# A state-space stage on one core: where the split of a quarter's result stands in the program

## The chip, the core and the metric

The kernel runs on one core of a Trainium2 chip as one launch. The metric is the device time of the whole kernel in microseconds (us). The engines are named as in the profile: PE (TensorE, matrix products), PEld (its weight loads), DVE (VectorE), ACT (ScalarE), POOL (GpSimd) and SP (SyncE, which here issues the DMAs). Each engine takes its instructions strictly in the order of its own list and waits where one is not ready; so an instruction that waits holds up all that stand behind it on that engine.

## The reference

One layer of a decoder trunk over 1024 tokens with 1024 channels, in float32. An input projection feeds three mixers side by side; their gated sum and a feed-forward part follow. Cut to what matters here:

```python
h = rms_norm(x, mix_norm_g[i])
(u, c_b, c_c, c_x, q, k_c, ..., mix_gates) = split_projection(h @ w_in[i])
y_ssm  = s5_mixer(u, ...)      # this change is inside the kernel's stage for it
y_conv = short_conv_mixer(c_x, c_b, c_c, conv_w[i], conv_w_out[i])
y_attn = nsa_mixer(q, ...)
mixed = gates[:, :, 0] * y_ssm + gates[:, :, 1] * y_conv + gates[:, :, 2] * y_attn

def s5_mixer(...):
    bu = einsum('bsgh,gph->bsgp', uf, b_bar)
    _, states = associative_scan(combine, (a, bu), axis=1)
    y = einsum('bsgp,ghp->bsgh', states, c).real + d_skip * uf
    y = gelu(y)
    y_lin, y_gate = split(y @ w_glu, 2)
    return y_lin * sigmoid(y_gate)
```

## The kernel before

Every float32 product is done as three products of two-part operands: a value is split into a rounded high part and a low remainder (`split`: the high part is one copy on ACT, line 61; the low part is one subtraction on DVE, line 62). In the trace these are `whi`, `wlo` for weights (from a page `raw` loaded by DMA) and `mhi`, `mlo` for moving operands. `prod` (lines 120, 122, 124) is the loop of three products. SBUF is cut into 44 pages of 128x1024 floats that are handed out in turn; a new holder of a page waits until the last reader of the old one is done. PE writes to four one-bank accumulators `acc` and two double ones `wide`.

The state-space mixer runs in four quarters of 128 channels, q = 0 to 3 (`s5`). A quarter, in the order of the program:

- `s5_kernel` (line 979 on): a short convolution kernel M, whose Toeplitz form is made by eight small DMAs `M<-kz` (line 991); `s5_carry`: four DMAs `cp<-cr`.
- `s5_back` (lines 1079 to 1085): the result of the quarter before, which `s5_out` had written to DRAM (`sy<-YN`), comes back transposed in eight DMAs `yT<-sy` (line 1084).
- `s5_inputs` (line 1002 on): eight transposes on PE and two copies on ACT make `Bm`.
- `s5_parts` (lines 1087 to 1091): the two-part split of `yT`, one ACT copy `mhi<-yT` and one DVE subtraction `mlo<-yT`. Its result is read only after all four quarters, by the products of `mix_ssm`.
- `s5_scan`: sixteen products `wide<-UT,Bm` (line 1015); copies of them into a page V, two on DVE (line 1024) and two on ACT (1022); then on DVE rotations and two rounds of four scans (lines 1031, 1033, 1035, 1039), and rotations back into `X` (lines 1048, 1050, 1054).
- `s5_tables` (lines 903 to 957) on DVE for the next quarter, and `s5_out`: products of M and of X (lines 1066, 1070) and a GELU on ACT (`YN`, line 1073).

Between these steps `beat` and `fill` put products of other mixers, one at a time, into PE's list: the short convolution (weights times `hh`, `hl`; evacuations `cb`, `z`, `cv` on ACT, products `z<-z,cb` and `cv<-cv,cy` on POOL, taps `cy` on DVE), then `u_block(3)` (the input of quarter 3), then `mix_plain` for the convolution branch (needs `mhi<-cv`, `mlo<-cv`; each accumulator is evacuated on DVE by line 1166, `m<-gp,acc`) and for the attention branch (needs `mhi<-oraw`, `mlo<-oraw`; evacuated as `gp<-gp,acc`). PE's order is written out by hand (`manual_schedule`); a list scheduler orders the other engines by program order and readiness.

```python
def s5_parts(self):
    hi, lo = self.page("mhi", F32R), self.page("mlo", F32R)
    cut = lambda x: x.rearrange("p (n t) -> p n t", t=8)
    self.split(cut(hi), cut(lo), self.last.rearrange("p t n -> p n t"))
    self.yT.append((hi, lo))
```

Of the kernel before, what the change touches and what calls it, by code (L numbers as in the profile page):

```python
# [33 lines left out]
class Trunk:  # L34
# [203 lines left out]
    def kv_rows(self):  # L238
# [7 lines left out]
        W = [self.weights() for _ in range(5)]  # L246
        A, B = (W[0], W[2]), (W[1], W[3], W[4])
        for t in range(NT):
            ps = self.wide()
            tok = slice(t * P, (t + 1) * P)  # L250
            for k in range(KD):
                a, b = A[k // 4], B[k // 3]
                ca, cb = slice((k % 4) * 256, (k % 4) * 256 + 256), slice((k % 3) * 280, (k % 3) * 280 + 280)
# [16 lines left out]
            nc.vector.tensor_tensor(sq[:, :256], kr, kr, op=OP.mult)  # L270
            nc.vector.tensor_reduce(self.ssk[:, t], sq[:, :256].rearrange("p (n d) -> p n d", d=64), axis=AX.X, op=OP.add)
            if t > 4:
# [34 lines left out]
    def q_rows(self):  # L307
# [3 lines left out]
        for t in range(NT):  # L311
# [8 lines left out]
            nc.vector.tensor_tensor(sq, q, q, op=OP.mult)  # L320
            nc.vector.tensor_reduce(self.ssq[:, t], sq.rearrange("p (n d) -> p n d", d=64), axis=AX.X, op=OP.add)
            self.q.append(q)
# [41 lines left out]
    def compress(self):  # L364
# [27 lines left out]
        for which in range(2):  # L392
# [25 lines left out]
            nc.vector.tensor_tensor(sv, kv, kv, op=OP.mult)  # L418
            nc.vector.tensor_reduce(ss, sv, axis=AX.X, op=OP.add)
            self.rstd(ss)  # L420
# [39 lines left out]
    def cmp_scores(self, t):  # L460
# [11 lines left out]
        m, sm = st[:, 0:8], st[:, 8:16]  # L472
        nc.vector.tensor_reduce(m, v, axis=AX.X, op=OP.max)
        nc.vector.tensor_tensor(v, v, m[:, :, None].to_broadcast([P, 8, 32]), op=OP.subtract)
        nc.scalar.activation(v, v, AF.Exp)
        nc.vector.tensor_tensor(v, v, self.seen[:, t, None, :].to_broadcast([P, 8, 32]), op=OP.mult)
        nc.vector.tensor_reduce(sm, v, axis=AX.X, op=OP.add)
        nc.vector.tensor_scalar(sm, sm, 1e-30, None, op0=OP.max)
# [199 lines left out]
    def u_block(self, q, beside=None):  # L678
# [9 lines left out]
        nc.sync.dma_start(spill, ut)  # L688
        self.U[q] = U = self.page("UT").rearrange("p (g n) -> p g n", g=8)
        nc.sync.dma_start(U, spill.rearrange("(g h) j n -> (h j) g n", g=8))  # L690

    def u_blocks(self):

        self.tab, self.U = {}, {}

# [299 lines left out]
    def s5_inputs(self, q, bp):  # L995

        nc = self.nc
        B = self.page("Bm").rearrange("p (a g c s) -> p a g c s", a=4, g=2, c=2)
        ps = self.wide()
# [4 lines left out]
        for c in range(2):  # L1004
            nc.scalar.activation(B[:, :, :, c], ps.rearrange("p (j c g s) -> p c j g s", j=4, c=2, g=2)[:, c], AF.Copy)
        self.fill(2 * self.F5)
        return B

    def s5_scan(self, q, U, B, ep):
        nc = self.nc  # L1010
        v = nc.vector
        V = self.page("V5").rearrange("p (c a n) -> p c a n", c=2, a=4)
        ps = self.wide()
        for j in range(8):
            nc.tensor.matmul(ps[:, j * P:(j + 1) * P], B[:, j // 2, j % 2].rearrange("p c s -> p (c s)"), U[:, j],
                             start=True, stop=True)
        pv = ps.rearrange("p (a g n) -> p g a n", a=4, g=2)
        for g in range(2):
            for c in range(2):
                o = V[g * 64:(g + 1) * 64, c]  # L1020
                if c:
                    nc.scalar.activation(o, pv[c * 64:(c + 1) * 64, g], AF.Copy)
                else:
                    nc.vector.tensor_copy(o, pv[c * 64:(c + 1) * 64, g])
        self.fill(2 * self.F5)
        f = lambda x: x.rearrange("p a n -> p (a n)")
        vr, vi, ec, es = f(V[:, 0]), f(V[:, 1]), f(ep[:, 0]), f(ep[:, 1])
        t = [self.half("m5") for _ in range(3)]
        a, b = self.half("a5"), self.half("b5")
        for o, z, x0, x1, op in ((b, t[2], vi, vr, OP.subtract), (a, t[0], vr, vi, OP.add)):  # L1030
            v.tensor_tensor(z, x0, ec, op=OP.mult)
            self.beat()
            v.tensor_tensor(t[1], x1, es, op=OP.mult)
            self.beat()
            v.tensor_tensor(z, z, t[1], op=op)
            self.beat()
            for j in range(4):
                s = slice(j * P, (j + 1) * P)
                v.tensor_tensor_scan(o[:, s], self.mag8[:, 4 * q + j:4 * q + j + 1].to_broadcast([P, P]), z[:, s], 0.0,
                                     op0=OP.mult, op1=OP.add)  # L1040
                if j % 2:
                    self.beat()
        X = self.page("X5").rearrange("p (a g n) -> p a g n", a=4, g=2)
        nc.gpsimd.memset(X[:, :, :, 0:1], 0.0)
        w = lambda x: x.rearrange("p (a n) -> p a n", a=4)[:, :, 0:127]
        ec, es = ep[:, 0, :, 0:127], ep[:, 1, :, 0:127]
        for c, x0, x1, op in ((0, a, b, OP.subtract), (1, b, a, OP.add)):
            v.tensor_tensor(w(t[0]), w(x0), ec, op=OP.mult)
            self.beat()
            v.tensor_tensor(w(t[1]), w(x1), es, op=OP.mult)  # L1050
            self.beat()
            for g in range(2):
                pr = slice(g * 64, g * 64 + 64)
                v.tensor_tensor(X[c * 64:(c + 1) * 64, :, g, 1:], w(t[0])[pr], w(t[1])[pr], op=op)
                self.beat()
        return X

    def s5_out(self, q, U, M, X, cp):

        nc = self.nc  # L1060
        Y = self.page("YN")
        ps = self.wide()
        for half in range(2):
            b = ps[:, half * 512:half * 512 + 512]
            for j in range(4):
                nc.tensor.matmul(b[:, j * P:(j + 1) * P], M[:, half * 2 + j // 2, j % 2], U[:, half * 4 + j],
                                 start=j == 0, stop=False, skip_group_check=True)
            for j in range(4):
                a, g = half * 2 + j // 2, j % 2
                nc.tensor.matmul(b[:, j * P:(j + 1) * P], cp[:, a, g], X[:, a, g], start=False, stop=j == 3,  # L1070
                                 skip_group_check=True)
            self.fill(self.F5)
        nc.scalar.activation(Y, ps, AF.Gelu_apprx_tanh)
        self.fill(2 * self.F5)
        self.spill_y = spill = self.dram.tile([P, 8, P], F32, tag=f"sy{q}", name=f"sy{q}")
        nc.sync.dma_start(spill, Y.rearrange("p (g n) -> p g n", g=8))
# [25 lines left out]
    def s5(self):  # L1102
        self.yT = []
        tab = self.tab
        for q in range(4):
            bp, cr, bb, ep = tab.pop(q)
            M = self.s5_kernel(q, cr, bb)
            cp = self.s5_carry(cr)
            U = self.U[q]
            if q:  # L1110
                self.s5_back()
            B = self.s5_inputs(q, bp)
            if q:
                self.s5_parts()
            self.F5B = 3.5 if q < 3 else 5
            X = self.s5_scan(q, U, B, ep)
            if q < 3:
                for _ in self.s5_tables(q + 1, tab):
                    self.beat()
            self.fill(self.F5S)  # L1120
            self.s5_out(q, U, M, X, cp)
        self.fill(16)
        self.s5_back()
        self.fill(16)
        self.s5_parts()
# [661 lines left out]
```

## Time and profile before

| | us |
|---|---|
| median of 3 runs (1775.83 to 1778.55) | 1776.4 |
| profiled execution: time | 1776.64 |
| profiled execution: span from first to last instruction | 1774.7 |
| PE busy in the span | 1736.4 (98%) |
| DVE busy | 1202.1 (68%) |
| ACT busy | 794.7 (45%) |

The profiled execution takes 1.9 us more than its span and stands 0.2 us above the median. PE is busy nearly all the time, so the time goes down only where PE waits or where its granted clock is at the lower of its two levels; mean granted clock 0.993 of full. A row of the timeline gives start, duration, engine, line, operation, operands, the count, and in brackets how long the engine was idle before it and what ended that.

### The profile page before, as it was taken

The numbers are of one execution on the slowest core, as the hardware profiler recorded it, in microseconds if no ns is written. First come the engines' busy times: TensorE is split into PE (matmuls) and PEld (weight loads), VectorE is DVE, ScalarE is ACT, GpSimd is POOL, SyncE is SP. The second block draws the span as 40 slices with busy tenths as digits, with TensorE's granted clock in tenths as the row PEclk, the third lists the DMA queues.
The fourth block names the chain that finished last, engine by engine and source line by source line (L and its number), as shares of the span: only waits on it lengthen the run. The fifth ranks groups of instructions, "written<-read, shape, count | busy, mean of one in ns | idle before, by whom it ended". The sixth has DMA issues, their size and how long they took to land.

```text
span 1774.7 us, 23597 instructions
## 1 busy us (share of the span) xinstructions
PE 1736.4 (98%) x8637; PEld 1437.0 (81%) x8637; DVE 1202.1 (68%) x2414; ACT 794.7 (45%) x1477; POOL 108.8 (6%) x94
## 2 busy tenths in 40 slices
PE   8999999999999999998979999999999999999999
PEld 7987788888888888887868888778888888888887
DVE  6975456667666674485675687698667776688681
ACT  6415567777777742233122234642323233244360
POOL 0000000000000010111000000002112211120000
PEclk9999999999999999999989999999999999999999
DMA  4213322221211224213636322433322332477531
GB/s 170 73 42 110 120 78 66 60 60 48 58 40 57 60 66 128 66 42 95 222 122 213 107 95 80 164 119 119 102 101 95 114 107 89 165 259 264 160 95 48
DMA packets 172665, 189.78 MB, mean 107 GB/s; under 512 B 16938, under 2 KB 129670, under 8 KB 172550
## 3 DMA queue, kind: packets, MB, share of 16 engines
q1 hardware_dynamic: 172517, 188.27, 33.1%
q8 instruction: 68, 1.11, 0.2%
q14 instruction: 48, 0.39, 0.1%
q10 hardware_dynamic: 32, 0.01, 0.0%
HBM read 134.50 MB, written 47.45 MB: 103 GB/s over the span
## 4 chain that ended last, share of the span: by engine, by line
PE 76%; DVE 12%; ACT 4%; issue 2%; SPq 2%; DMA 2%; POOL 1%; POOLq 0%; ACTq 0%; DVEq 0%
PE wide L1517 11%; PE acc L120 10%; PE acc L124 10%; PE acc L122 10%; PE acc L1517 7%; PE acc L1624 5%; PE wide L1624 5%; PE acc L560 3%; PE wide L519 3%; PE acc L1286 2%; DVE A L62 2%; PE wide L1286 2%; PE acc L583 2%; PE acc L582 2%; PE wide L257 1%
## 5 line engine op out<-in xcount | busy, mean ns | idle before, releaser
L120 PE MATMUL acc<-hh,whi 128*128 128x512 f32 x672 | 269.6, 401 | 4.8 <-ACT whi L61 3.3
L124 PE MATMUL acc<-hh,wlo 128*128 128x512 f32 x672 | 268.3, 399 | 1.7 <-DVE wlo L62 1.7
L122 PE MATMUL acc<-hl,whi 128*128 128x512 f32 x672 | 268.8, 400 | 0.0
L1517 PE MATMUL wide<-B,A 128*128 128x512 f32 x1056 | 250.7, 391 | 0.3
L1517 PEld LDWEIGHTS wide<-B,A 128*128 128x128 f32 x1056 | 196.6, 188 | 47.1 <-DVE sg L1530 3.3
L1517 PE MATMUL acc<-B,A 128*128 128x512 f32 x792 | 192.0, 393 | 2.6 <-ACT A L61 1.6
L1517 PEld LDWEIGHTS acc<-B,A 128*128 128x128 f32 x792 | 148.8, 189 | 35.6 <-ACT A L61 2.4
L120 PEld LDWEIGHTS acc<-hh,whi 128*128 128x128 f32 x672 | 127.1, 189 | 26.0 <-ACT whi L61 3.7
L124 PEld LDWEIGHTS acc<-hh,wlo 128*128 128x128 f32 x672 | 127.3, 189 | 22.2 <-DVE wlo L62 2.8
L122 PEld LDWEIGHTS acc<-hl,whi 128*128 128x128 f32 x672 | 127.1, 189 | 19.6 <-issue 0.2
L61 ACT ACTIVATE A<-S 128x512 fp32r<-128x512 f32 x88 | 54.8, 627 | 164.7 <-DVE S L1449 164.0
L62 DVE TENSOR_TENSOR ptl<-acc,pth 128x512 fp32r<-128x512 f32 (+1 forms) x152 | 93.8, 619 | 50.3 <-ACT pth L61 49.1
L1624 PE MATMUL acc<-wdp,act 128*128 128x512 f32 x528 | 121.5, 389 | 0.6 <-DVE wdp L62 0.6
L524 DVE CUSTOM_DVE_ANT_0 p<-wide,mask 128x640 f32<-128x640 f32 (+7 forms) x128 | 90.1, 704 | 43.2 <-PE wide L519 40.5
L62 DVE TENSOR_TENSOR wlo<-raw,whi 128x1024 fp32r<-128x1024 f32 (+1 forms) x75 | 90.5, 1210 | 40.0 <-ACT whi L61 24.4
L1624 PEld LDWEIGHTS acc<-wdp,act 128*128 128x128 f32 x528 | 99.0, 188 | 21.7 <-DVE wdp L62 1.0
L1473 POOL TENSOR_TENSOR sg<-sg 128x512 f32<-128x512 f32 x44 | 73.9, 1680 | 598.2 <-ACT A L61 520.4
L527 ACT ACTIVATE p<-p,small 128x640 f32<-128x640 f32 (+7 forms) x128 | 93.6, 731 | 37.0 <-DVE small L524 34.9
L120 PE MATMUL acc<-mhi,whi 128*128 128x512 f32 x256 | 101.8, 398 | 7.3 <-DVE m L1166 7.3
L122 PE MATMUL acc<-mlo,whi 128*128 128x512 f32 x256 | 101.8, 398 | 4.1 <-DVE mlo L62 4.1
L61 ACT ACTIVATE pth<-acc 128x512 fp32r<-128x512 f32 (+1 forms) x152 | 80.9, 534 | 46.0 <-PE acc L560 45.4
L124 PE MATMUL acc<-mhi,wlo 128*128 128x512 f32 x256 | 101.3, 396 | 0.0
(397 smaller groups left out, 3246.1 us busy)
## 6 DMA issues: line engine op xcount, KB each, us to landing
raw<-in_ffn_w_gate_up_dram SPq DMA_DIRECT2D x52, 512.0 KB
raw<-in_w_in_dram SPq DMA_DIRECT2D x48, 512.0 KB
sa<-sg SPq DMA_DIRECT2D x77, 256.0 KB
araw<-sa SPq DMA_DIRECT2D x77, 256.0 KB
sg<-tg SPq DMA_DIRECT2D x48, 256.0 KB
gp<-sg SPq DMA_DIRECT2D x24, 512.0 KB
x<-in_x_dram SPq DMA_DIRECT2D x16, 512.0 KB
wd<-in_ffn_w_down_dram SPq DMA_DIRECT2D x11, 512.0 KB
```

Source lines behind the costliest of these rows:

```text
L61: self.nc.scalar.activation(hi, src, AF.Copy)
L62: self.nc.vector.tensor_tensor(lo, src, hi.bitcast(F32), op=OP.subtract)
L120: self.nc.tensor.matmul(out, hi(k), mh(k), start=start and j == 0, stop=False)
L122: self.nc.tensor.matmul(out, hi(k), ml(k), start=False, stop=False)
L124: self.nc.tensor.matmul(out, lo(k), mh(k), start=False, stop=stop and j == n - 1)
L519: nc.tensor.matmul(ps[:, c * 512:c * 512 + w], self.QS[t][:, h], k[:, k0 + c * w:k0 + c * w + w], start=z == 0, stop=z == 1)
L524: nc.vector.tensor_tensor_reduce(p[:, :n].rearrange("p (c w) -> p c w", c=pieces), v, m.rearrange("p (c w) -> p c w", c=pieces), scale=-1. ...
L527: nc.scalar.activation(p[:, :n], p[:, :n], AF.Exp, scale=-1.0, bias=st[:, hh:hh + 1], accum_out=st[:, 2 + hh:3 + hh])
L1286: nc.tensor.matmul(ps, act[:, x * 512 + t * P:x * 512 + (t + 1) * P], w[:, y * 512:y * 512 + 512], start=i == 0 and j == 0 and p in (1, 5, ...
L1473: e.tensor_tensor(o, x, y, op=op)
L1517: nc.tensor.matmul(ps, x, y, start=p in (1, 5, 6, 7) and k + j == 0, stop=k == 3 and j == 2, skip_group_check=True)
L1624: nc.tensor.matmul(ps, act[:, x * 512 + t * P:x * 512 + (t + 1) * P], w[:, y * 512:y * 512 + 512], start=i == 0 and j == 0 and p in (1, 5, ...
```

## The change

In quarters 1 to 3 the split of the result of the quarter before (`s5_parts`) no longer stands ahead of the scan stage: it is called inside `s5_scan`, behind its two rounds of scans and ahead of the rotations back into X. The transposed read from DRAM (`s5_back`) is called after `s5_inputs` instead of before it. The last split, after quarter 3, stays where it was. No operation is added or removed.

```diff
                                      op0=OP.mult, op1=OP.add)
                 if j % 2:
                     self.beat()
+        if q:
+            self.s5_parts()
         X = self.page("X5").rearrange("p (a g n) -> p a g n", a=4, g=2)
...
             M = self.s5_kernel(q, cr, bb)
             cp = self.s5_carry(cr)
             U = self.U[q]
+            B = self.s5_inputs(q, bp)
             if q:
                 self.s5_back()
-            B = self.s5_inputs(q, bp)
-            if q:
-                self.s5_parts()
             self.F5B = 3.5 if q < 3 else 5
             X = self.s5_scan(q, U, B, ep)
```

The lists of PE and SP come out in the same order as before (line numbers behind 1042 are two higher). Those of ACT and DVE change. ACT in quarter 2, before, from the copy of z's second half on; `whi<-raw` in the fourth row is the weight of `u_block(3)`, and in brackets are the counters that an instruction waits for (DMAHW0 to 7 count DMAs):

```order
L722 ACTIVATE z<-acc 128x512 [waits PE_49]
L61 ACTIVATE mhi<-yT 128x1024 [waits DMAHW4_49,DMAHW3_49,DMAHW5_49,DMAHW2_49,DMAHW6_49,DMAHW1_49,DMAHW7_49,DMAHW0_49,Activation_49]
L727 ACTIVATE cy<-z,par 128x1024 [waits Pool_49]
L1022 ACTIVATE V_8415<-wide 64x512 [waits DVE_49]
L61 ACTIVATE whi<-raw 128x1024
L1022 ACTIVATE V_8415<-wide 64x512 [waits DVE_49]
L732 ACTIVATE cv<-acc 128x512 [waits PE_49] x2
L61 ACTIVATE mhi<-cv 128x1024 [waits Pool_49]
L61 ACTIVATE whi<-raw 128x1024
L683 ACTIVATE ut<-acc 128x8x64 [waits DVE_49,PE_49]
```

ACT there now:

```order
L722 ACTIVATE z<-acc 128x512 [waits PE_49]
L1022 ACTIVATE V_8411<-wide 64x512 [waits DMAHW4_49,DVE_49,Activation_49]
L727 ACTIVATE cy<-z,par 128x1024 [waits Pool_49]
L1022 ACTIVATE V_8411<-wide 64x512 [waits DVE_49]
L61 ACTIVATE whi<-raw 128x1024 [waits DMAHW4_49,DMAHW5_49,DMAHW3_49,DMAHW6_49,DMAHW2_49,DMAHW7_49,DMAHW1_49,DMAHW0_49]
L732 ACTIVATE cv<-acc 128x512 [waits PE_49]
L61 ACTIVATE mhi<-yT 128x1024 [waits DMAHW4_49,DMAHW5_49,DMAHW3_49,DMAHW6_49,DMAHW2_49,DMAHW7_49,DMAHW1_49,DMAHW0_49]
L732 ACTIVATE cv<-acc 128x512 [waits PE_49]
L61 ACTIVATE mhi<-cv 128x1024 [waits Pool_49]
L61 ACTIVATE whi<-raw 128x1024
```

The split of yT has moved behind the copies of V, cy, `whi` and the first half of cv. `whi<-raw` now waits for eight DMA counters itself, where before it had none.

DVE in quarter 2, before, from the split of yT on (V, m, b and a are the scan's tiles, cy the convolution's taps):

```order
L62 TENSOR_TENSOR mlo<-yT,mhi 128x1024
L1024 COPY V_8415<-wide 64x512
L728 SCALAR_TENSOR_TENSOR cy<-z,par,cy 128x1023
L1024 COPY V_8415<-wide 64x512
L729 SCALAR_TENSOR_TENSOR cy<-z,par,cy 128x1022
L62 TENSOR_TENSOR wlo<-raw,whi 128x1024
L1031 TENSOR_TENSOR m_8459<-V_8415,ep 128x512
L1033 TENSOR_TENSOR m_8458<-V_8415,ep 128x512
L1035 TENSOR_TENSOR m_8459<-m_8459,m_8458 128x512
L1039 SCALAR_TENSOR_TENSOR b_8461<-mag_765,m_8459 128x128 x4
L1031 TENSOR_TENSOR m_8457<-V_8415,ep 128x512
L1033 TENSOR_TENSOR m_8458<-V_8415,ep 128x512
```

DVE there now:

```order
L1024 COPY V_8411<-wide 64x512 x2
L728 SCALAR_TENSOR_TENSOR cy<-z,par,cy 128x1023
L1031 TENSOR_TENSOR m_8455<-V_8411,ep 128x512
L729 SCALAR_TENSOR_TENSOR cy<-z,par,cy 128x1022
L62 TENSOR_TENSOR wlo<-raw,whi 128x1024
L1033 TENSOR_TENSOR m_8454<-V_8411,ep 128x512
L62 TENSOR_TENSOR mlo<-yT,mhi 128x1024
L1035 TENSOR_TENSOR m_8455<-m_8455,m_8454 128x512
L1039 SCALAR_TENSOR_TENSOR b_8457<-mag_765,m_8455 128x128 x4
L1031 TENSOR_TENSOR m_8453<-V_8411,ep 128x512
L1033 TENSOR_TENSOR m_8454<-V_8411,ep 128x512
L1035 TENSOR_TENSOR m_8453<-m_8453,m_8454 128x512
```

`mlo<-yT` has moved from the head of this stretch to behind V, cy, `wlo` and two rotations, ahead of the scans.

DVE in quarter 3, before, beside the products for the convolution and attention branches:

```order
L1166 SCALAR_TENSOR_TENSOR m<-gp,acc 128x512 x2
L62 TENSOR_TENSOR mlo<-yT,mhi 128x1024
L1024 COPY V_8918<-wide 64x512
L62 TENSOR_TENSOR mlo<-oraw,mhi 128x1024
L1024 COPY V_8918<-wide 64x512
L62 TENSOR_TENSOR wlo<-raw,whi 128x1024
L1031 TENSOR_TENSOR m_8965<-V_8918,ep 128x512
L1166 SCALAR_TENSOR_TENSOR m<-gp,acc 128x512
L1033 TENSOR_TENSOR m_8964<-V_8918,ep 128x512
L1166 SCALAR_TENSOR_TENSOR m<-gp,acc 128x512
L1035 TENSOR_TENSOR m_8965<-m_8965,m_8964 128x512
L62 TENSOR_TENSOR mlo<-oraw,mhi 128x1024
```

DVE there now:

```order
L1166 SCALAR_TENSOR_TENSOR m<-gp,acc 128x512
L1024 COPY V_8914<-wide 64x512
L1166 SCALAR_TENSOR_TENSOR m<-gp,acc 128x512
L1024 COPY V_8914<-wide 64x512
L62 TENSOR_TENSOR mlo<-oraw,mhi 128x1024
L62 TENSOR_TENSOR wlo<-raw,whi 128x1024
L1031 TENSOR_TENSOR m_8961<-V_8914,ep 128x512
L1033 TENSOR_TENSOR m_8960<-V_8914,ep 128x512
L1166 SCALAR_TENSOR_TENSOR m<-gp,acc 128x512
L1035 TENSOR_TENSOR m_8961<-m_8961,m_8960 128x512
L1166 SCALAR_TENSOR_TENSOR m<-gp,acc 128x512
L62 TENSOR_TENSOR mlo<-oraw,mhi 128x1024
```

Here `mlo<-yT` is gone from between the evacuations (line 1166) and V; V's copies now stand among the evacuations. It comes a little later, between the scans of `a` and X:

```order
L62 TENSOR_TENSOR wlo<-raw,whi 128x1024
L1039 SCALAR_TENSOR_TENSOR a_8962<-mag_765,m_8959 128x128 x4
L1166 SCALAR_TENSOR_TENSOR gp<-gp,acc 128x512
L1050 TENSOR_TENSOR m_8959<-a_8962,ep 128x4x127
L62 TENSOR_TENSOR mlo<-yT,mhi 128x1024
L1052 TENSOR_TENSOR m_8960<-b_8963,ep 128x4x127
L1166 SCALAR_TENSOR_TENSOR gp<-gp,acc 128x512
L1056 TENSOR_TENSOR X_9061<-m_8959,m_8960 64x4x127
```

In quarter 3 X now stands behind `mlo<-yT`, which stands behind the first evacuation of the attention branch.

## Rows read from the trace of the kernel before

**Rows 1.** Windows: sum, busy PE, PEld, DVE, ACT, POOL, then granted clock, DMA share, GB/s.

```profile
750.00:760.00 10.00, 10.00 (x46) 8.29 (x45) 0.88 (x1) 3.06 (x3) 2.40 (x1) 1.00 0.65 180
...
820.00:830.00 10.00, 5.00 (x18) 3.31 (x17) 7.72 (x7) 6.31 (x7) 1.50 (x1) 0.83 0.11 40
```

**Rows 2.** Timeline, ACT, quarters 2 and 3: start, duration, operation, idle before and its releaser.

```profile
820.13 2.05 ACT L61 ACTIVATE mhi<-yT 128x1024 fp32r<-128x1024 f32 x1 [7.25 <-DMA yT<-sy]
822.09 1.14 ACT L727 ACTIVATE cy<-z,par 128x1024 f32<-128x1024 f32 x1
...
825.31 1.04 ACT L61 ACTIVATE whi<-raw 128x1024 fp32r<-128x1024 f32 x1
...
892.53 2.06 ACT L61 ACTIVATE mhi<-yT 128x1024 fp32r<-128x1024 f32 x1 [13.43 <-DMA yT<-sy]
```

**Rows 3.** Timeline, PE, quarter 2: around its two stops.

```profile
822.06 0.39 PE L124 MATMUL acc<-hh,wlo 128*128 128x512 f32 x1
...
822.74 0.39 PE L124 MATMUL acc<-hh,wlo 128*128 128x512 f32 x1
826.40 0.64 PE L120 MATMUL acc<-hh,whi 128*128 128x512 f32 x1 [3.28 <-ACT whi L61]
...
829.19 0.79 PE L124 MATMUL acc<-hh,wlo 128*128 128x512 f32 x1 [1.72 <-DVE wlo L62]
...
833.55 0.40 PE L120 MATMUL acc<-hh,whi 128*128 128x512 f32 x1
...
853.88 0.47 PE L120 MATMUL acc<-mhi,whi 128*128 128x512 f32 x1 [1.08 <-DVE m L1166]
```

**Rows 4.** Timeline, PE, quarter 3: around its two stops.

```profile
895.04 0.39 PE L124 MATMUL acc<-mhi,wlo 128*128 128x512 f32 x1
901.63 0.77 PE L120 MATMUL acc<-mhi,whi 128*128 128x512 f32 x1 [6.20 <-DVE m L1166]
...
905.39 0.40 PE L120 MATMUL acc<-mhi,whi 128*128 128x512 f32 x1
909.87 0.79 PE L122 MATMUL acc<-mlo,whi 128*128 128x512 f32 x1 [4.08 <-DVE mlo L62]
...
915.48 0.40 PE L124 MATMUL acc<-mhi,wlo 128*128 128x512 f32 x1
...
926.81 1.06 PE L1070 MATMUL wide<-X,cp 128*128 128x128 f32 x8
```

**Rows 5.** Timeline, PE: products of the inputs, quarters 2 and 3.

```profile
809.61 1.95 PE L1015 MATMUL wide<-UT,Bm 128*128 128x128 f32 x16
...
881.46 1.95 PE L1015 MATMUL wide<-UT,Bm 128*128 128x128 f32 x16
```

**Rows 6.** Timeline, POOL, quarter 2.

```profile
812.96 2.39 POOL L726 TENSOR_TENSOR z<-z,cb 128x1024 f32<-128x1024 f32 x1 [17.44 <-ACT z L722]
...
828.50 2.86 POOL L734 TENSOR_TENSOR cv<-cv,cy 128x1024 f32<-128x1024 f32 x1 [12.97 <-ACT cv L732]
```

**Rows 7.** Timeline, DVE, quarter 2.

```profile
822.21 1.98 DVE L62 TENSOR_TENSOR mlo<-yT,mhi 128x1024 fp32r<-128x1024 f32 x1 [18.13 <-ACT mhi L61]
...
829.05 2.85 DVE L1031 TENSOR_TENSOR m<-V,ep 128x512 f32<-128x512 f32 x1
...
834.60 0.66 DVE L1031 TENSOR_TENSOR m<-V,ep 128x512 f32<-128x512 f32 x1
...
853.04 0.69 DVE L1166 SCALAR_TENSOR_TENSOR m<-gp,acc 128x512 f32<-128x512 f32 x1
```

**Rows 8.** Timeline, DVE, quarter 3.

```profile
894.62 1.97 DVE L62 TENSOR_TENSOR mlo<-yT,mhi 128x1024 fp32r<-128x1024 f32 x1 [9.34 <-ACT mhi L61]
896.51 0.67 DVE L1024 COPY V<-wide 64x512 f32<-64x512 f32 x1
...
908.60 1.21 DVE L62 TENSOR_TENSOR mlo<-oraw,mhi 128x1024 fp32r<-128x1024 f32 x1
...
922.10 1.40 DVE L1054 TENSOR_TENSOR X<-m,m 64x508 f32<-64x508 f32 x2
```

## The prediction

> **What bounds the kernel now.** I read the summary table first: PE is busy 98% of the span, so the change can only give back the little time in which PE waits or runs at the lower clock. I then read what PE waits for, over the whole program: nearly all its long waits lie inside the state-space stage, in quarters 2 and 3, and in one evacuation right behind quarter 2. The timeline of PE gives their size, those of ACT and DVE their cause.
>
> At full clock PE starts three matmuls in 0.68 us, from 822.06 to 822.74 [rows 3], so 0.227 us for one.
>
> Quarter 2: the matmul behind 822.74 is due at 822.97 and starts at 826.40, after 3.28 us of idleness that `whi` on ACT ends; a second wait, for `wlo` on DVE, ends at 829.19, and PE is back at speed at 833.55 [rows 3]. In the window 820 to 830 PE was granted a mean clock of 0.83 [rows 1], so part of it ran at 1.2 GHz instead of 2.4. From 826.40 up to 833.55 stand 12 matmuls, worth 2.72 us. So what starts at 833.55 was due at 825.69: **7.86 us lost**. A third wait of 1.08 us, for an evacuation on DVE, ends at 853.88 [rows 3].
>
> Quarter 3: due at 895.27, started at 901.63 after 6.20 us, stopped again for 4.08 us before 909.87, at speed again at 915.48 [rows 4]. Between lie 10 and 13 matmuls, worth 5.2 us: due at 900.5, **15.0 us lost**.
>
> The cause is one instruction in each quarter. ACT's `mhi<-yT` starts at 820.13 in quarter 2, after 7.25 us of idleness that the DMA ends, and at 892.53 in quarter 3, after 13.43 us [rows 2]. Behind it on ACT stands the very `whi` that PE waits for: it runs at 825.31 [rows 2]. On DVE `mlo<-yT` waits for `mhi`: 18.13 us idle before 822.21 [rows 7] and 9.34 us before 894.62 [rows 8], and behind it stand the copies of V, `wlo`, and in quarter 3 the evacuations for want of which PE has no free accumulator. In quarter 1 the same head of the queue costs nothing: PE is busy 10.00 of 10 us from 750 to 760 although DVE is busy only 0.88 [rows 1], since its weights are split well ahead there.
>
> **The change part by part.** No operation comes or goes; the orders of PE and SP are the same. So the read of yT is issued and lands as before, at about 820.1 and 892.5 (the starts of `mhi<-yT`) [rows 2]; moving `s5_back` behind `s5_inputs` is worth 0: it issues the same eight DMAs at the same place of SP's list, past no other. What changes is who stands behind that landing. I follow each quarter on the clock of before, and shift nothing until PE gains.
>
> Quarter 2. The products of the inputs end at 809.61 + 1.95 = 811.6 [rows 5]; V is copied then, where it waited until 824 before. The taps cy need POOL's `z<-z,cb`, which ends at 812.96 + 2.39 = 815.35 [rows 6], and 1.14 us of ACT [rows 2]: 816.5. Two short ACT instructions behind it comes `whi`, 1.04 us long [rows 2]: done at about 818.1. It now waits for eight DMAs; if these are copies of M, issued early in the quarter, that is nothing, if they were the pieces of yT it is done at 820.1 + 1.04 = 821.2. Both are before 822.97. `wlo` follows on DVE at 820 to 822.4; PE wants it two matmuls in, at 823.4. So both waits of quarter 2 go: 7.86 us, and PE enters `u_block(3)` at 822.97.
>
> But DVE does not get ahead by as much as PE does. Before, it went without a pause from 822.21 to the first evacuation at 853.04: 30.83 us [rows 7]. The same work, less two copies of V (0.67 us each [rows 8]) and begun at 816.5 with cy, ends at 846.0; on its way `mlo<-yT` waits for `mhi<-yT` (820.13 + 2.05 [rows 2] = 822.2, where DVE arrives at about 821.5): 0.7 more, **846.7**. PE restarts 0.84 us after the evacuation begins (853.04 [rows 7] to 853.88 [rows 3]): 847.5. By then PE has done the 48 matmuls of `u_block(3)` and the 48 that fill four accumulators (twelve each), and stands from 822.97 + 96 x 0.227 = 844.8. So a wait of about 2.7 us stays where 1.08 was, and the quarter gives 853.88 - 847.5 = **6.4 us**, not 7.86.
>
> In the 30.83 us is one DVE row of 2.85 us whose twin takes 0.66 [rows 7]; it lies beside POOL's `cv<-cv,cy` of 2.86 us [rows 6]. I keep it in the sum, as that product still falls into busy DVE time; without it the evacuation is 2.2 us earlier and the quarter gives 8.6. "SBUF — State Buffer" of the Trainium skill, section "SBUF: two separate sides", says that VectorE and GpSimd share one port pair, held for a whole instruction, so that the loser fully blocks. These two rows agree with it; it speaks against this quarter, whose DVE work is now laid beside that product again, and by it the sum stays at 6.4.
>
> Quarter 3. The products of the inputs end at 881.46 + 1.95 = 883.4 [rows 5]. From V's first copy at 896.51 to the end of the last `mlo<-oraw` at 908.60 + 1.21 = 909.81 DVE needed 13.3 us [rows 8]. Now the stretch starts at 883.4, with V's two copies parted by an evacuation, so perhaps 0.5 us of waiting, and with 0.6 us less before its end, since one rotation moves behind it: it ends at 896.6 or earlier. PE wants that low part ten matmuls into the attention branch (before, the stop behind 905.39 [rows 4]): 895.27 + 2.27 = 897.5. Free accumulators come from evacuations that now run as their products end, the latest of those PE needs at about 891. So both stops go: 15.0 us. The work that now hides `mhi<-yT` is the evacuating itself; were V's copies late, the old stop would return.
>
> What is late next is X. Before, DVE went from 909.81 to the end of X at 922.10 + 1.40 = 923.5 [rows 8]: 13.7 us. Now `mlo<-yT` (1.97 us [rows 8]) and 1.3 us of evacuation and rotation are added, and some 1.9 us in which it waited for PE fall away: X ends at about 896.6 + 15.1 = 911.7. PE wants it in line 1070, before at 926.81 [rows 4], without the loss at 911.8. That is no margin; I take 0.4 us for it, with bounds of 0 and 1.5.
>
> Sum: 6.4 + 15.0 - 0.4 = **21.0 us**. Against the profiled execution, 1776.64 - 21.0 = 1755.6; that stands 0.2 above the median, so 1755.4 for a median.
>
> **The rivals.**
>
> *The clock falls in the wait that stays.* After 3.28 us of idleness PE came back at the lower clock, after 1.08 us it did not [rows 3]; 2.7 us lies nearer to the first. The price: the 13 matmuls from 909.87 to 915.48 took 5.61 us instead of 2.95 [rows 4], 2.7 us. Against it: the estimate of 2.7 us holds work that may overlap. "TensorE: Matmul & The Clock Gate" of the Trainium skill, section "What's actually happening", says that the clock is set by how busy the array has been of late and that the slow level is what idleness brings; the halved rate behind 826.40 and 909.87 agrees. With this 1758.1.
>
> *All is given back.* POOL's product meets nothing, the wait behind quarter 2 vanishes: 7.86 + 1.2 + 15.0 = 24.1, so 1752.3.
>
> *Quarter 3 keeps a stop.* Its two margins, 0.9 us for `mlo<-oraw` and none for X, are thin. If DVE comes 3 us later than I reckon (for a DMA of the gates or of `oraw` that lands late, or a page not yet free), PE waits 2 to 3 us and loses 2.7 to the clock: 1761. With both rivals' losses 1764.
>
> *Nothing moves.* `whi` or V waits for a page whose reader stands behind the same landing, so that DVE starts at 822 and 892 as before: 1776. The eight counters in front of `whi` are the only place where I see such a wait, and its later bound still precedes PE's need.
>
> *Slower.* X now stands behind `mlo<-yT`, so if yT lands late PE waits in line 1070 of the same quarter, where before it had some of its slack. DVE comes to that split at about 901.8 in quarter 3; with 2.05 us for `mhi` yT must land by 899.7, and it landed at 892.5. To eat the 21 us and 3.6 more it would have to land at 924, 32 us later, from a queue that has not changed.
>
> **How the numbers follow.** Forecast (no lower clock in quarter 2, no stop in quarter 3, 1754 to 1757): 0.50. Lower clock: 0.20. All given back: 0.08. Quarter 3 keeps a stop, alone or with the clock: 0.16. Nothing moves: 0.04. Slower: 0.02. Predicted 1755.4. The range runs from the second rival, 1752.3 less half a microsecond for the spread of runs, to 1763.5, which takes in most of the third: it leaves out the last two rivals and the tail of the third, about 0.1. A difference under 0.2% (3.6 us) can hardly be told from none here; every case but the last two is faster by more: faster 0.94, same 0.04, slower 0.02.
>
> **What would show it.** In the trace after: V's copies on DVE right behind the products of the inputs, with a wait for PE and not for ACT; `mhi<-yT` in quarters 2 and 3 with no or under 3 us of idleness before it; no wait of PE for `whi` or `wlo` ahead of `u_block(3)`; one wait for line 1166 of 2 to 3 us some 22 us later; no stop at the start of the attention branch; granted clock 1.00 in quarter 3. The step that I trust least is the 30.83 us carried over as one block: if DVE loses time to POOL at two places, the wait grows to 5 us with a fall of the clock. The prediction is wrong if quarter 3 shows a wait on `mlo<-oraw` or X of more than 2 us.

## The result and the profile after

| | before | changed |
|---|---|---|
| median, us | 1776.12 (1774.62 to 1778.55) | 1753.29 (1752.09 to 1753.43) |
| ratio, 95% interval | | 0.9869 (0.9852 to 0.9886) |
| profiled execution: time / span, us | 1776.64 / 1774.7 | 1753.43 / 1751.5 |
| mean granted clock | 0.993 | 0.999 |

The change takes 22.8 us; 21.0 were forecast, and 1753.29 lies within the range of 1751.8 to 1763.5, 2.1 us below the single number. The waits of PE over the whole program, after (in total, times, longest, in us), show first what is gone:

```profile
PE acc L120 <- DVE m L1166: 1.8, 1, 1.8
...
PE acc L122 <- DVE wlo L62: 0.6, 2, 0.4
PE acc L124 <- DVE wlo L62: 0.3, 1, 0.3
```

Of the five stops of [rows 3] and [rows 4] one is left, the evacuation wait behind quarter 2; the second row here is elsewhere and was there before, and the third is a small new stop, at 834.00 below. The timeline of PE, after, shows this wait and the places by which the gain can be divided:

```profile
808.86 1.95 PE L1015 MATMUL wide<-UT,Bm 128*128 128x128 f32 x16
...
834.00 0.50 PE L124 MATMUL acc<-mhi,wlo 128*128 128x512 f32 x1 [0.29 <-DVE wlo L62]
...
844.34 0.39 PE L124 MATMUL acc<-mhi,wlo 128*128 128x512 f32 x1
846.53 0.47 PE L120 MATMUL acc<-mhi,whi 128*128 128x512 f32 x1 [1.81 <-DVE m L1166]
...
847.86 0.63 PE L124 MATMUL acc<-mhi,wlo 128*128 128x512 f32 x1
848.28 0.63 PE L120 MATMUL acc<-mhi,whi 128*128 128x512 f32 x1
...
875.49 1.95 PE L1015 MATMUL wide<-UT,Bm 128*128 128x128 f32 x16
...
905.83 1.06 PE L1072 MATMUL wide<-X,cp 128*128 128x128 f32 x8
```

PE's list is the same, so distances between the same instructions can be compared. From the products of the inputs of quarter 1 (747.05 before, 746.30 after) to those of quarter 2 it is 62.56 us in both, so quarter 1 gives nothing. From the products of the inputs of quarter 2 to those of quarter 3 it was 71.85 us [rows 5] and is 66.63: **5.2 us** gained. From there to the first product of X it was 45.35 [rows 4, 5] and is 30.34: **15.0 us**. Ahead of 808.86 lie another 0.75 us and behind X 2.2 (1774.7 - 926.81 = 847.9 against 1751.5 - 905.83 = 845.7); the four make the 23.2 us of the span.

ACT's timeline, after, beside [rows 2]:

```profile
814.64 1.15 ACT L727 ACTIVATE cy<-z,par 128x1024 f32<-128x1024 f32 x1 [1.89 <-POOL z L726]
815.82 0.60 ACT L1022 ACTIVATE V<-wide 64x512 f32<-64x512 f32 x1
816.44 1.06 ACT L61 ACTIVATE whi<-raw 128x1024 fp32r<-128x1024 f32 x1
817.52 0.60 ACT L732 ACTIVATE cv<-acc 128x512 f32<-128x512 f32 x1
818.89 2.11 ACT L61 ACTIVATE mhi<-yT 128x1024 fp32r<-128x1024 f32 x1 [0.76 <-DMA yT<-sy]
...
888.60 2.12 ACT L61 ACTIVATE mhi<-yT 128x1024 fp32r<-128x1024 f32 x1 [0.30 <-PE acc L122]
```

`whi`, which stood behind the landing until 825.31, now runs at 816.44 with no idle time before it: its eight counters cost nothing. Of 7.25 and 13.43 us of waiting for `yT` 0.76 and none are left. DVE and POOL after, beside [rows 6 to 8]:

```profile
821.03 2.03 DVE L62 TENSOR_TENSOR mlo<-yT,mhi 128x1024 fp32r<-128x1024 f32 x1 [0.39 <-ACT mhi L61]
...
823.69 3.45 DVE L1039 TENSOR_TENSOR_SCAN b<-mag,m 128x128 f32<-128x128 f32 x4
...
829.12 1.37 DVE L1039 TENSOR_TENSOR_SCAN a<-mag,m 128x128 f32<-128x128 f32 x4
...
845.71 0.68 DVE L1166 SCALAR_TENSOR_TENSOR m<-gp,acc 128x512 f32<-128x512 f32 x1
...
877.47 0.68 DVE L1024 COPY V<-wide 64x512 f32<-64x512 f32 x1 [2.69 <-PE wide L1015]
...
889.53 1.22 DVE L62 TENSOR_TENSOR mlo<-oraw,mhi 128x1024 fp32r<-128x1024 f32 x1
...
903.63 1.40 DVE L1056 TENSOR_TENSOR X<-m,m 64x508 f32<-64x508 f32 x2
```

```profile
823.09 2.81 POOL L734 TENSOR_TENSOR cv<-cv,cy 128x1024 f32<-128x1024 f32 x1 [8.32 <-DVE mlo L62]
```

Four scans beside POOL's product take 3.45 us, their twins without it 1.37. X ends at 905.03, 0.8 us before line 1072 wants it. Windows of 10 us, after (columns as in [rows 1]):

```profile
750.00:760.00 10.00, 10.00 (x46) 8.29 (x45) 9.24 (x15) 5.69 (x7) 4.72 (x7) 1.00 0.60 170
820.00:830.00 10.00, 10.00 (x46) 8.29 (x45) 9.51 (x14) 4.11 (x5) 4.52 (x6) 1.00 0.19 63
...
840.00:850.00 10.00, 8.19 (x32) 6.31 (x31) 9.85 (x18) 1.06 (x1) 0.00 (x0) 0.88 1.06 390
850.00:860.00 10.00, 10.00 (x52) 8.54 (x51) 7.82 (x17) 0.00 (x0) 0.46 (x1) 0.95 0.68 259
...
890.00:900.00 10.00, 10.00 (x46) 8.29 (x45) 10.00 (x15) 1.67 (x2) 0.01 (x1) 1.00 1.02 355
900.00:910.00 10.00, 10.00 (x60) 8.82 (x59) 9.70 (x13) 0.00 (x0) 0.00 (x0) 1.00 0.10 40
```

The window 820 to 830 has gone from half busy at a clock of 0.83 to full at 1.00. From 750 to 760, in quarter 1, DVE does 9.24 us of work instead of 0.88, and PE was and is full. In these windows the clock drops only behind 846.53.

### The profile page after: what moved, and what is told of

Its sections match the earlier page's. It is cut to its first block, busy times and chain, and to the rows that moved or that the text cites. A ratio compares the mean times of both kernels' runs of the same rounds, so it can differ in the third digit from the quotient of the medians.

```text
span 1751.5 us, 23611 instructions
## 1 busy us (share of the span) xinstructions
PE 1728.9 (99%) x8637; PEld 1433.2 (82%) x8637; DVE 1202.8 (69%) x2414; ACT 795.4 (45%) x1477; POOL 108.8 (6%) x94
## 4 chain that ended last, share of the span: by engine, by line
PE 86%; DVE 6%; ACT 4%; issue 1%; DMA 1%; SPq 1%; POOL 0%; POOLq 0%; ACTq 0%; DVEq 0%
PE wide L1517 13%; PE acc L124 12%; PE acc L120 12%; PE acc L122 11%; PE acc L1517 9%; PE acc L1624 6%; PE wide L1624 5%; PE acc L560 3%; PE wide L519 3%; PE acc L1286 2%; PE wide L1286 2%; PE acc L583 2%; PE acc L582 2%; PE wide L257 1%; PE wide L256 1%
## 5 line engine op out<-in xcount | busy, mean ns | idle before, releaser
L120 PEld LDWEIGHTS acc<-hh,whi 128*128 128x128 f32 x672 | 126.6, 188 | 22.3 <-issue 2.2
```

What stands on the lines that cost most here:

```text
L120: self.nc.tensor.matmul(out, hi(k), mh(k), start=start and j == 0, stop=False)
```

## The experiments

Four groups: which line of the change acts, whether the landing of `yT` is the cause, what each quarter is worth, and what is left behind quarter 2. Each run was timed beside the kernel before on the same chip.

**Which part acts.** The read alone behind the input's products (`s5_back` moved, the split at its old place):

```diff
-            if q:
-                self.s5_back()
             B = self.s5_inputs(q, bp)
             if q:
+                self.s5_back()
                 self.s5_parts()
```

> Only the read of yT moves behind s5_inputs; the split stays ahead of the scan stage. Theory of the landing (the split at the head of ACT's and DVE's lists waits for yT's DMA): the eight DMAs are issued at the same place of SP's list, so nothing moves: 1776, within 3 us of the kernel before, PE again stops for some 3 us in quarter 2 and 6 + 4 us in quarter 3. Rival, the read's place is what pays: 1755.

Measured 1775.74 us against 1776.61, ratio 0.9998 (0.9988 to 1.0007). The waits of PE in this kernel (as above) are the stops of [rows 3] and [rows 4], each within 1.2 us of its size there:

```profile
PE acc L120 <- DVE m L1165: 8.3, 2, 7.3
...
PE acc L122 <- DVE mlo L62: 3.6, 1, 3.6
PE acc L120 <- ACT whi L61: 3.1, 1, 3.1
PE acc L124 <- DVE wlo L62: 1.8, 1, 1.8
```

And the split alone behind the scan's loops, the read at its old place:

```diff
+        if q:
+            self.s5_parts()
         X = self.page("X5").rearrange("p (a g n) -> p a g n", a=4, g=2)
...
             B = self.s5_inputs(q, bp)
-            if q:
-                self.s5_parts()
```

> Only the split moves behind the scans; the read of yT stays ahead of s5_inputs. Theory of the landing: the whole gain, 1753 to 1756, with one wait of about 2 us for line 1166 left. Rival, the read's place pays: 1776.

Measured 1755.45 us (1753.02 to 1760.32), ratio 0.9887 (0.9869 to 0.9906), which overlaps with the whole change's. So the gain comes from the split's place, and the read's place is worth nothing that can be told in the time; the profile with the read at its old place has one wait that the changed kernel's has not, 0.76 us for `mlo` in quarter 3.

**Is the landing the cause?** First the kernel before, with the split at its old place reading the tile `UT`, which is there already, instead of `yT` in quarters 1 to 3; so those three results are replaced by other data:

```diff
-    def s5_parts(self):
+    def s5_parts(self, early=None):
...
-        self.split(cut(hi), cut(lo), self.last.rearrange("p t n -> p n t"))
+        self.split(cut(hi), cut(lo), (self.last if early is None else early).rearrange("p t n -> p n t"))
...
-                self.s5_parts()
+                self.s5_parts(U.rearrange("p g n -> p g n"))
```

> Kernel before, with the split at its old place ahead of the scan, but in quarters 1 to 3 it reads the quarter's own input page UT, which landed long ago, in place of yT (so the branch's result is of other data; yT is still read back, and nobody uses it). The split's work stays at the head, only its wait for the DMA goes. Theory of the landing: most of the gain, 1753 to 1758; the 2 us of split on ACT and DVE come before V then, where DVE is idle anyway. Rival, it is the 4 us of split work in a full stretch and not the wait: 1770 to 1776.

Measured 1756.29 us (1754.97 to 1756.87), ratio 0.9888 (0.9873 to 0.9902). The order of before without the landing gives 20.3 of the 22.8 us. Its distances (line 1015 of quarter 2 starts at 809.13) say where, in the timeline of PE and DVE of this kernel:

```profile
872.41 1.95 PE L1015 MATMUL wide<-UT,Bm 128*128 128x128 f32 x16
...
879.74 1.23 DVE L62 TENSOR_TENSOR mlo<-oraw,mhi 128x1024 fp32r<-128x1024 f32 x1 [4.59 <-DMA cp<-cr]
...
891.92 0.80 PE L122 MATMUL acc<-mlo,whi 128*128 128x512 f32 x1 [2.61 <-DVE mlo L62]
...
909.12 1.06 PE L1070 MATMUL wide<-X,cp 128*128 128x128 f32 x8
```

From quarter 2 to quarter 3 it is 63.28 us, 8.6 less than before and so more than the change gets there. From there to X it is 36.71, also 8.6 less, where the change gets 15.0: PE keeps one long wait, for the low part of `oraw`, and DVE had stood 4.59 us ahead of one of these low parts for what the profile gives as a DMA of `cp`. So the landing is all of the loss in quarter 2 and over half of it in quarter 3. Whether the rest there is this other wait or the place of the split, no run separates.

Second, again the order of before and its own data, but the read issued earlier in SP's list, ahead of the DMAs of M and `cp`:

```diff
             bp, cr, bb, ep = tab.pop(q)
+            if q:
+                self.s5_back()
             M = self.s5_kernel(q, cr, bb)
             cp = self.s5_carry(cr)
             U = self.U[q]
-            if q:
-                self.s5_back()
```

> Kernel before, but the read of yT is issued ahead of the eight copies of M and the four of cp (ahead of s5_kernel); the split stays at its old place ahead of the scan. Theory of the landing: yT lands about 8 us earlier in quarters 2 and 3, near 811 and 879, before V's products end, so the waits of PE go as with the change: 1753 to 1760. M and cp come 5 us later and still 30 us before PE needs them. Rival, the place of the split in the lists matters whatever it waits for: 1770 or more.

Measured 1758.64 us (1757.80 to 1759.63), ratio 0.9902 (0.9887 to 0.9917). ACT's timeline of this kernel:

```profile
807.70 2.02 ACT L61 ACTIVATE mhi<-yT 128x1024 fp32r<-128x1024 f32 x1 [1.46 <-DMA M<-kz]
811.28 0.60 ACT L722 ACTIVATE z<-acc 128x512 f32<-128x512 f32 x1 [1.57 <-PE acc L124]
814.63 0.59 ACT L1022 ACTIVATE V<-wide 64x512 f32<-64x512 f32 x1 [2.75 <-DMA cp<-cr]
```

The split runs 12.4 us earlier than in [rows 2], where 8 were expected, and the stops at `whi` and `wlo` are gone. So most of the gain can be had by moving the read past twelve DMAs instead of moving the split; but then those twelve land later, the copy of V waits 2.75 us for what the profile gives as a DMA of `cp<-cr`, and PE keeps waits of 1.2 us behind quarter 2 and of 2.60 us in quarter 3. No run moves the copy on ACT without the subtraction on DVE, so what each of the two holds back by itself is not shown.

**What each quarter is worth.** The change in quarter 2 alone and in quarter 3 alone; the read stands behind the input's products in both (an edit of the changed kernel):

```diff
-        if q:
+        if q == 2:
             self.s5_parts()
...
             if q:
                 self.s5_back()
+                if q != 2:
+                    self.s5_parts()
```

> The split moves behind the scans in quarter 2 alone; in quarters 1 and 3 it stays ahead of the scan. Landing theory, with the two losses of the sum: quarter 2 gives 6 to 7 us, quarter 3 keeps its stops of 6 and 4 us: 1769 to 1771. Rival, the gain of quarter 3 hangs on quarter 2 (DVE gets ahead there): 1760 or less.

> The split moves behind the scans in quarter 3 alone. Landing theory: quarter 3 gives 15 us, quarter 2 keeps its stops of 3.3 and 1.7 us: 1760 to 1763. Rival as in the run for quarter 2 alone: less than 10 us gained, 1767 or more.

Measured beside 1775.59 us: quarter 2 alone 1769.53, ratio 0.9968 (0.9956 to 0.9980), so 6.1 us; quarter 3 alone (the same lines with 3) 1759.35, ratio 0.9910 (0.9895 to 0.9925), 16.2 us. Timeline of PE, quarter 2 alone:

```profile
847.29 0.47 PE L120 MATMUL acc<-mhi,whi 128*128 128x512 f32 x1 [1.77 <-DVE m L1168]
895.94 0.77 PE L120 MATMUL acc<-mhi,whi 128*128 128x512 f32 x1 [7.10 <-DVE m L1168]
904.19 0.79 PE L122 MATMUL acc<-mlo,whi 128*128 128x512 f32 x1 [3.64 <-DVE mlo L62]
```

The stops of quarter 3 stay where quarter 3 keeps its order. Quarter 3 alone came out 0.65 us below the range expected of it. The two gains, forecast at 6.4 and 14.6, add to 22.3 us of the change's 22.8, with intervals of 2 to 3 us on each; so neither is seen to take from the other, and nothing is left over for quarter 1.

**What is left behind quarter 2.** Two edits of the changed kernel: the split moved further back, behind the next quarter's tables, so that its 2 us lie behind the first evacuation; and POOL's product for the branch's last column block (c = 3) on DVE instead:

```diff
-        if q:
-            self.s5_parts()
...
+            if q:
+                self.s5_parts()
```

> As the change, but the split stands behind s5_tables instead of behind the scans, so in quarter 2 its 2 us of DVE come after the first evacuations of the convolution branch. Theory of the wait that stays (DVE's block of work up to the first evacuation at line 1166 is what is late): that block is 2.4 us shorter, the wait of 1.8 us goes, and with it a spell at the lower clock of 3.4 us (1.7 us): 1749 to 1751. Rival, a page that yT holds longer delays the fetch of a gate page and with it the evacuation: 1755 or more.

```diff
-                    nc.gpsimd.tensor_tensor(cv, cv, cy, op=OP.mult)
+                    (nc.gpsimd if c < 3 else nc.vector).tensor_tensor(cv, cv, cy, op=OP.mult)
```

> As the change, but the last product cv<-cv,cy (column block 3) runs on DVE instead of POOL. If DVE's lost 2.1 us beside that product come from POOL (the scans of b took 3.45 us beside it and 1.37 us for a), DVE pays 1.2 us for the product itself and saves 2.1: the wait of 1.8 us falls to about 0.9 and the lower clock with it: 1750 to 1752.5. If the long row has another cause, DVE has 1.2 us more to do: the wait grows to 3 us, 1754 to 1757.

The later split: 1751.26 us, ratio 0.9865 (0.9850 to 0.9880), 0.3 us above the range of its theory and well below its rival. The product on DVE: 1752.11, ratio 0.9872 (0.9855 to 0.9888). DVE with the later split:

```profile
821.95 1.37 DVE L1039 TENSOR_TENSOR_SCAN b<-mag,m 128x128 f32<-128x128 f32 x4
...
823.83 2.88 DVE L1033 TENSOR_TENSOR m<-V,ep 128x512 f32<-128x512 f32 x1
...
844.31 0.71 DVE L1166 SCALAR_TENSOR_TENSOR m<-gp,acc 128x512 f32<-128x512 f32 x1
```

DVE with the product moved to it:

```profile
824.51 1.37 DVE L1039 TENSOR_TENSOR_SCAN b<-mag,m 128x128 f32<-128x128 f32 x4
...
827.71 1.22 DVE L734 TENSOR_TENSOR cv<-cv,cy 128x1024 f32<-128x1024 f32 x1
...
845.36 0.69 DVE L1166 SCALAR_TENSOR_TENSOR m<-gp,acc 128x512 f32<-128x512 f32 x1
```

With the later split the scan is short again, but the multiplication that now lies beside POOL takes 2.88 us instead of 0.68: the loss goes to whichever of these DVE instructions comes next beside the product. Not every one loses: in the changed kernel a copy of V (at 812.79, 0.69 us) lies within POOL's `z<-z,cb` (812.21 to 814.60) and takes no longer than elsewhere. With the product on DVE it is gone from both, for 1.22 us of DVE's own. PE's wait behind quarter 2 is 0.5 and 1.2 us instead of 1.8. Neither interval is apart from the change's, so the three were run beside each other: both edits together, the change again, and the later split again.

> The split stands behind the next quarter's tables, and the second-half product cv of the convolution is on VectorE instead of GpSimd. Theory (what is left to gain is the wait of PE behind quarter 2 and the lower clock that it can bring): each part alone already takes most of that away, so the two together add nothing that can be told: 1750 to 1752.5, no wait for line 1166 or its neighbour over 0.5 us. Rival (the two parts remove different losses, 2.0 and 1.2 us): 1748.5 to 1750.

> The change itself, unaltered, beside the other two on one chip. If the part moved further back really gains, this stands 1.5 to 2.5 us above the late split (1752.5 to 1754 against 1750.5 to 1752); if the difference seen so far is that of chips and runs, the two stand within 1 us of each other. Its wait behind quarter 2 is 1.8 us again in both cases; the spell of lower clock behind it, 3.4 us once and absent with the same wait in the run with the split alone, tells whether that spell is a matter of the execution.

> The split behind the next quarter's tables, again. If it gains over the change: 1750.5 to 1752, below the change on the same chip by 1.5 us or more. If not: within 1 us of it.

| beside 1775.04 us | us | single times | ratio, 95% |
|---|---|---|---|
| the change again | 1753.78 | 1752.92 to 1753.98 | 0.9881 (0.9866 to 0.9895) |
| later split again | 1751.94 | 1750.71 to 1752.49 | 0.9870 (0.9854 to 0.9887) |
| later split, product on DVE | 1750.07 | 1749.17 to 1752.13 | 0.9862 (0.9848 to 0.9877) |

The four times of the change lie above all eight of the other two, so some 1.8 and 3.7 us below it are likely real, though the intervals of the ratios overlap and 0.2% is near what can be told. With both edits PE waits for no evacuation behind quarter 2; this is the fastest version run. Its time alone does not say whether the 1.9 us below the later split are real, nor which of the two expectations for it is right: 1750.07 lies where they meet. The distances on PE, from the products of the inputs of quarter 2 to those of quarter 3 and from there to the first product of X, say more:

| kernel (profiles) | quarter 2 to 3, us | quarter 3 to X, us |
|---|---|---|
| before | 71.85 | 45.35 |
| quarter 2 alone | 65.21 | 45.27 |
| quarter 3 alone | 71.32 | 30.34 |
| the change (two) | 66.63, 65.24 | 30.34, 30.35 |
| split alone, read at its old place | 65.19 | 31.39 |
| split at its old place, reading `UT` | 63.28 | 36.71 |
| split at its old place, read issued earlier | 64.04 | 35.57 |
| product on DVE | 64.06 | 30.34 |
| later split (two) | 63.30, 63.30 | 30.34, 30.34 |
| later split, product on DVE | 62.33 | 30.34 |

Against the change's 65.24 the later split takes off 1.9 us, in both its profiles, the product on DVE 1.2, and both together 2.9. So the two parts remove different losses, as the rival expectation had it, and about 1.0 of the 1.9 us is seen in the trace, of one profile.

## Why the prediction was right

**Right: the mechanism.** One instruction that waits for the landing stood at the head of ACT's and DVE's lists. Taking the landing away without moving anything gives 20.3 us, and an earlier read 18.0. In quarter 2 the landing is the whole loss; in quarter 3 these two runs give back 8.6 and 9.8 of the 15.0 us, so there it is the larger part and not shown to be all. That moving `s5_back` is worth nothing is shown by the read alone, and that quarter 1 is by its unchanged 62.56 us.

**Right: the places of quarter 2.** On the clock after, 0.75 us earlier, the prediction puts the end of cy on ACT at 815.75, the first evacuation at 845.95 and PE's restart at 846.75. Measured: 814.64 + 1.15 = 815.79, 845.71 and 846.53. So the 30.83 us carried over as one block, the step I trusted least, held to 0.2 us, with the collision kept in it. The 0.2 is the wait for `mhi<-yT`, 0.39 us for the 0.7 reckoned; the rest of the block, from DVE's start on cy at 815.83, took the 29.5 us that the prediction gave it. By "SBUF — State Buffer" of the Trainium skill, section "SBUF: two separate sides", a VectorE instruction with two inputs in SBUF that meets a GpSimd one on the shared port pair stays blocked to the other's end; the trace agrees: the scans begun at 823.69 lose 2.1 us, and POOL's product ends 2.2 us after they begin.

**Mis-sized: the wait that stays, and the clock.** "A wait of about 2.7 us stays": it was 1.81, or 1.96 counted as the prediction counts, from when the next matmul was due (844.57). Of the 0.7 us between them 0.5 is not gain, since PE came to the place that much later than reckoned (844.57 against 844.05), after the small stop for `wlo` at 834.00 that the prediction had not. At the restart PE stood 853.88 - 0.75 - 846.53 = 6.6 us earlier, for 6.4 forecast. Then the first rival came true in part: from 847.86 on seven matmuls ran at half the rate, 0.63 us each and 0.42 us apart, and the quarter ended with 5.2. In the second profile of the same kernel, with the same wait, they did not, and the quarter's distance is 65.24 us, a gain of 6.6. So that rival's price, 2.7 us, was 1.4 here, and it is paid in some executions and not in others.

**Right in sum, with a thinner margin than it looks: quarter 3.** Forecast 15.0 less 0.4; measured 15.0. The last `mlo<-oraw` was forecast to end at 896.6 on the clock of before, of which 6.0 us (0.75 and 5.2) are gained by then: 890.6; it ended at 889.53 + 1.22 = 890.75. X, by the same step due at 905.7, ended at 905.03, 0.8 us before PE wanted it, so the 0.4 was not paid. The rival in which quarter 3 keeps a stop did not occur in the change, but the runs with the split at its old place and no late landing show it: the 2.6 us for `mlo<-oraw`.

**Missed: what lies outside the two quarters.** The terms add to 20.2 us measured against 21.0 forecast; the profiled executions differ by 23.2. The 0.75 us ahead of quarter 2's products is there already at the products of quarter 0 (684.73 us before, 683.98 after), ahead of every line that the change touches. Of the 2.2 behind X some 1.4 is a stretch at the lower clock that the profile of before has and the one of after has not: twelve products of line 1517 take 4.50 us there and 3.08 after (windows of before):

```profile
1140.00:1150.00 10.00, 7.80 (x32) 5.98 (x32) 6.85 (x12) 5.65 (x11) 0.00 (x0) 0.83 0.07 26
```

The later split's second profile has the same stretch at the same two waits (1.20 and 1.00 us), so it isn't the change that takes it away. From the first product of X to the end the thirteen profiles of this document take 845.2 to 848.1 us, and the longest is one of the later split. I had compared one execution with the sum of the terms and made no allowance for this. Timed a second time, beside another run of before, the change gives 1775.04 - 1753.78 = 21.3 us, nearer to the forecast.

## What to carry to other kernels

Where an engine with an in-order list idles for a DMA, look first at who stands behind the waiting instruction and whether its result is needed soon; if it isn't, moving it behind the work that others wait for gives back most of the stop (here 5.2 to 6.6 of 7.9 us in quarter 2 and 15.0 of 15.0 in quarter 3), and reading earlier gives nearly as much (18.0 of 22.8). Moving it further back still took another 1.9 us off quarter 2. Size such a gain from the engine that is waited for: follow its list from the new start as one block of measured length, and see where the bounding engine stands next. Then measure the distance between the same instructions before and after, since the ends of two profiled executions can differ by some 3 us for other reasons, as they did here.

## What the runs showed of the hardware

The clock after a wait isn't settled by the wait's length. Behind 1.8 us of idleness at the same place PE fell to the lower level in one profile of the changed kernel (windows above, 0.88 and 0.95) and not in another (windows of the second run of it):

```profile
840.00:850.00 10.00, 8.19 (x37) 6.49 (x36) 9.82 (x16) 1.07 (x1) 0.00 (x0) 1.00 0.94 340
850.00:860.00 10.00, 10.00 (x56) 8.39 (x55) 9.08 (x20) 0.00 (x0) 0.46 (x1) 1.00 0.91 342
```

Behind 2.6 us it came back at the lower level at once in the run without the landing (0.80 us for the first matmul), and in the run with the earlier read it started at full rate and fell 1.05 us later (first matmul 0.50 us; mean clock 0.66 and 0.83 in the window 890 to 900):

```profile
892.15 0.50 PE L122 MATMUL acc<-mlo,whi 128*128 128x512 f32 x1 [2.60 <-DVE mlo L62]
...
893.20 0.63 PE L124 MATMUL acc<-mhi,wlo 128*128 128x512 f32 x1
```

"TensorE: Matmul & The Clock Gate" of the Trainium skill, section "What's actually happening", says that the clock follows how busy the array has been of late; the traces agree in that each fall looked at here stands behind idleness, and show that a wait of this size decides it neither way.
